# Gate and up projections: weight loads that read every second word in half of the contraction groups

## The chip, the cores and the metric

The kernel runs on one core of a Trainium2 chip. The metric is the device time of one execution, in microseconds (us). The kernel before takes 2003.84 us, the median of 2 runs (2003.69 and 2003.99). The engines are named as in the profile: PE is the matrix engine TensorE, PEld its weight loads, DVE the VectorE, ACT the ScalarE, POOL the GpSimd, SP the SyncE, which here only issues transfers.

## The reference

One layer of a decoder trunk with 512 tokens and 2048 features, all in float32: a norm, an input projection, two groups of attention heads side by side, an output projection, a residual sum, and then the part that this case is about, a gated feed-forward block with 5632 inner features.

```python
def _swiglu(h, w_gate, w_up, w_down):
    return (jax.nn.silu(h @ w_gate) * (h @ w_up)) @ w_down

def reference(x, ...):
    for l in range(DEPTH):
        h = _rms_norm(x, attn_norm[l])
        x = x + _hybrid_mixer(h, ...)
        h = _rms_norm(x, ffn_norm[l])
        x = x + _swiglu(h, w_gate[l], w_up[l], w_down[l])
    return x
```

Here `w_gate` and `w_up` are 2048 x 5632 and `w_down` is 5632 x 2048.

## The kernel before

**Products.** Each float32 operand is cut into a high and a low part by ScalarE (a copy that rounds) and VectorE (the difference), and a product of two operands is taken as three products on TensorE: high by high, high by low, low by high. Gate, up and down also use a scheme with seven products of sums of blocks in place of eight products of blocks (a Strassen-like scheme), so the operands are "forms", seven sums of blocks each.

**Gate and up.** The output features of each of the two matrices are cut into 22 pairs of blocks of 128 (`NJ`, index `j`), and the 2048 features that are summed over into 4 contraction groups (`NG`, index `g`). For each `j`, first gate and then up (`which`) runs over its four groups. Step `i` stands for one group, so there are 22 x 2 x 4 = 176 steps. The weights of a step come from HBM in one transfer of 512 KB into a tile `r`, as four blocks of 256 words on each of 128 partitions: two halves (`kk`) of 128 words each, one behind the other. VectorE adds the blocks to the forms (`sums`), and ScalarE and VectorE write the high and low parts of all seven forms into the tile `bigm` (`part_steps`), at one of two places in turn. The activations' forms lie ready for the whole stage: the program names them forma for group 0, formx for group 1, formy for group 2, and for group 3 they lie in bigm as well.

A step then makes 42 matmuls: for the high part of the weights 2 halves x 7 forms x 2 (the activations' high and low part), and for the low part 2 halves x 7 forms. Each has 256 tokens as its columns, and each is preceded by a weight load of its own, 128 x 128, even where two matmuls in a row use the same weights. In the profile a matmul is PE, its load PEld. The weights are the stationary operand:

```python
cs = slice(kk * P, (kk + 1) * P)
...
mm(o, w[wp][:, fb, cs], a[:, xp, fa], ...
```

The helper `mm` (line 412) reads the moving operand not one column after the other, but in turn from the two halves of the block: column 0, column 128, column 1, column 129 and so on. Attention's products (`mm3`) call the engine directly and read their columns one after another. No stationary operand is read in any other way than word after word.

The results gather in four PSUM tiles `q`. After four steps they are put together by VectorE and ScalarE (`evict`, `gate_out`, `up_out`) while the next matrix is running, and the finished blocks go to HBM for the last stage.

**Down** follows as the last stage, with 512 columns in each matmul (tiles `pd`).

**Order of the work.** Up to the start of the second pair of gate the order on each engine is written out in a table (`ORDERS`); behind it the program's own order holds. TensorE runs the steps one after the other; the sums and the parts of a step are made one and two steps ahead, and the transfers are issued three to four steps ahead on SP.

**The functions and their use.** `_blocks` lays out the two matrices on the host, `kernel` calls it, and `hybrid_layer` holds the loop.

Of the kernel before, what the change touches and what calls it, by code (L numbers as in the profile page):

```python
# [18 lines left out]
P = 128  # L19
# [9 lines left out]
NG = 4  # L29
# [204 lines left out]
def hybrid_layer(ctx: ExitStack, tc: tile.TileContext, xT, vec, ffb, wfg, wfirst, win, cmpw, wout, wos, wgu, wdn, out):  # L234
# [109 lines left out]
    def split(dst, src, scale=None, neg=None):  # L344

        if scale is None:
            h = act(dst[:, 0], src, AF.Copy)
            tt(dst[:, 1], src, dst[:, 0].bitcast(F32), op=OP.subtract)
            return h
        else:  # L350
            sca.activation(dst[:, 0], src, AF.Copy, scale=scale)
            dve.scalar_tensor_tensor(dst[:, 1], src, scale, dst[:, 0].bitcast(F32),
                                           op0=OP.mult, op1=OP.subtract)
# [14 lines left out]
    def high_tile(name):  # L368
        return wpl.tile([P, HALF * P], FR, tag="wh", name=name, bufs=2)
# [42 lines left out]
    def mm(o, w, x, j=1, **kw):  # L412
        pe.matmul(_like(o, j), w, _in_turn(x, j), **kw)
# [17 lines left out]
    def stagger(*gens, lag=LAG):  # L431

        for g in gens:
            for i, mark in enumerate(g):
                if mark is POST:
                    run(late[0])
                    late[0] = g
                    break
                if i >= lag and i % 2 == 0:
                    next(late[0], None)  # L440
                yield

    def run(steps):
        for _ in steps:
            pass
# [603 lines left out]
    def chain(*gens):  # L1049
        for g in gens:  # L1050
            yield from g
# [12 lines left out]
    for k in range(NK):  # L1064
# [5 lines left out]
        wp = high_tile(f"w0p_{k}")[:, :2 * T].rearrange("p (s c) -> p s c", s=2)  # L1070
# [134 lines left out]
    def fetch(at):  # L1205
        key = next(wanted, None)
        if key is None:
            if at < 3:
                ws_turn.append(at)
            return  # L1210
        n, f = key
        while emitted[0] < GROUP * (n // 2 + 1):
            sum_weights(highs[-1], osums)
            emitted[0] += 1
        i = FIRST7 + 2 * n
        src = {0: win[i, 0], 1: win[i, 1], 6: win[i + 1, 1]}.get(f)
        if src is None:
            src = fsum[PAIRS[n]][{4: 0, 3: 1, 5: 2, 2: 3}[f]].rearrange("p i c -> p (i c)")
        fetched[key] = ws_tile(f"pair{n}_{f}", at), at
        load(fetched[key][0], src)  # L1220
# [156 lines left out]
    for n, p in enumerate(PAIRS[:-1]):  # L1377
        g = stagger((pair if p[0] == "p" else vpair)(p[1]), lag=LAG7)
# [67 lines left out]
    def x1_steps(n, z, place=None, formed=False):  # L1446

        xr = ftile(f"xr{n}") if place is None else oxp.tile([P, T], F32, tag="ox", name=f"xr{n}", bufs=OXB)
        load(xr, xT[n])
        t, sq = (ftile(f"x1_{n}"), xr) if place is None else (xr, place)  # L1450
        yield
        tt(_apart(t, 2), _mixed(z[0], 2), _apart(xr, 2), op=OP.add)
        pin(sca.dma_start(x1d[n], t)) if n == NK - 1 else pool.dma_start(x1d[n], t)
        yield
        if formed:
            raw_forms(n, t)
        add_squares()
        act(sq, t, AF.Square)
        squared.append((n, sq))
        if formed:  # L1460
            yield
            add_squares()
        yield
# [112 lines left out]
    for i, n in enumerate((0, HALF)):  # L1576
        g = x1_steps(n, both_z[i:])
# [3 lines left out]
    for n, tag, at in ((5, "g", 4),):  # L1581
        z = [None, tag]
        pieces += [one_tile(n, z, j) for j in range(2)]
        g = x1_steps(n, z)
# [15 lines left out]
    def seven_out(p):  # L1600

        n = SEVEN[p]
        c = [oxp.tile([P, T], F32, tag="ox", name=f"c7_{n}{i}", bufs=OXB) for i in range(2)]
        xs = [x1_steps(n + HALF * i, c[i:], c[i]) for i in range(2)]
        for x in xs:
            next(x)
        yield
        steps = put_together(qs[p], c, ftile(f"e7_{n}"))
        next(steps)
        yield  # L1610
        next(steps)
        yield
        run(steps)
        next(xs[0])
        yield
        next(xs[1])
        yield
        next(xs[0])
        yield
        next(xs[1])  # L1620
        yield

    for g in order7:
        at = len(pieces)
        pieces += g
        if g in others:
            p = others.index(g)
            o = seven_out(p)
# [7 lines left out]
    for i, n in enumerate((5 + HALF, 6, 6 + HALF, 7, 7 + HALF)):  # L1636
# [3 lines left out]
        def tail(n=n, z=z):  # L1640
            x = x1_steps(n, z, formed=(n % HALF == 7))
            if n == 7 + HALF:
                live["x1s"] = x
            next(x)
            yield
            next(x)
            yield
            if n == 7:
                next(x)
                live["raw7"] = live["raw"]  # L1650
            next(x)
            yield

        g = tail()
# [139 lines left out]
    ORDER = list(range(2 * NJ * NG))  # L1794
# [14 lines left out]
    def sums(i):  # L1809
        r = raws[i]  # L1810
        tt(r[:, 4:6], r[:, 1:3], r[:, 0:1].to_broadcast([P, 2, 256]), op=OP.add)
        tt(r[:, 6], r[:, 4], r[:, 2], op=OP.add)
        tt(r[:, 7], r[:, 6], r[:, 3], op=OP.add)
# [14 lines left out]
    def parts(i):  # L1828
        run(part_steps(i))
# [79 lines left out]
    def load_a(i):  # L1909
        second, j = pass_of(i)[1:]  # L1910
        at = (8 + 2 * (turn[1] % 3)) * T
        turn[1] += 1
        rawa[i] = cut(live["fa"], at, (3 if second else 4) * 256)
        d = fetch2(rawa[i], ad[j][:, 4:7] if second else ad[j][:, 0:4])
        if i == 2:
            tc.add_manual_dep(d.ins, live["w0"].ins.name, PACE)
# [53 lines left out]
    for j in range(NJ):  # L1970
        for which in range(2):
            q = [ps.tile([P, T], F32, tag=tag, name=f"q{which}{j}_{i}", bufs=BUFS[tag])
                 for i, tag in enumerate(SETS[which])]
            for g in range(NG):
                i = (2 * j + which) * NG + g

                if 3 <= i < LAST - 1:
                    sums(i + 2)
                if 3 <= i < LAST:
                    parts(i + 1)  # L1980
                    fetch(i + 4)
                if i == 4:
                    split(fr2, acc)
                if i == LAST - 2:
                    live["fa"] = ffp.tile([P, 2 * FORM + OFF_FORM], F32, tag="fa", name="rawm", bufs=1)
                    for n in range(2):
                        load_a(n)
                        run(load_w(n))
                w = split_w.pop(i)
                if j == 1 and which == 0 and g == 0:  # L1990
                    close_order(tc, engines)

                for wp in range(2):
                    for kk in range(2):
                        k = 2 * (ORDER[i] % NG) + kk
                        a = forms[k]
                        cs = slice(kk * P, (kk + 1) * P)
                        for fa, fb, b, h in PROD:
                            o = q[b][:, h * 256:(h + 1) * 256]
                            for xp in range(2 - wp):  # L2000
                                mm(o, w[wp][:, fb, cs], a[:, xp, fa],
                                   start=(k == 0 and h == 0 and wp == 0 and xp == 0),
                                   stop=(g == NG - 1 and kk == 1 and wp == 1), skip_group_check=True)
                if i == 0:
                    sums(2)
                    form_sums(live["raw"])
                    parts(2)
                    sums(3)
                    form_parts(HALF - 1, live["raw"])
                elif i == 1:  # L2010
                    sums(4)
                    parts(3)
                    run(x1s)
                    fetch(5)
                elif i == 2:
                    fetch(6)
                if j == 0 and which == 1 and g == 1:
                    row_rstd2([sets[0][3][:, 256:512], q[3][:, 256:512]])
                next(pending, None)
                if g == 1 and j > 0:  # L2020
                    next(turning, None)
                if i >= LAST - 1:
                    ahead[i - LAST + 1] = splits(i - LAST + 1)
            sets = [q]
            pending = chain(pending, (up_out if which else gate_out)(j, q))
# [94 lines left out]
    for ps_ in range(4):  # L2120
        p, second = ps_ // 2, ps_ % 2
# [71 lines left out]
        pending = chain(*ends)  # L2193


def _in_turn(x, j=1):

    return x.rearrange("p (j b a) -> p j a b", j=j, b=2)


def _like(x, j=1):

    return x.rearrange("p (j a b) -> p j a b", j=j, b=2)
# [24 lines left out]
def _blocks(w, np):  # L2228

    w = w.reshape(2, NG, 2, P, -1, 2, P)  # L2230
    w = np.stack([w[0, ..., 1, :], w[0, ..., 0, :], w[1, ..., 1, :], w[1, ..., 0, :]])
    return np.ascontiguousarray(w.transpose(4, 1, 3, 0, 2, 5)).reshape(-1, NG, P, 4 * 2 * P)
# [75 lines left out]
```

## Time and profile before

| | |
|---|---|
| median of the timed runs | 2003.84 us |
| the profiled execution | 2001.04 us, of which its span is 1999.3 us |
| granted TensorE clock | 1.0 |
| PE busy | 1989.7 us (100% of the span), 14413 matmuls |
| PEld busy | 1883.6 us (94%), 14413 loads |
| DVE busy | 1783.7 us (89%) |
| ACT busy | 1098.6 us (55%) |
| POOL busy | 332.8 us (17%) |
| matmuls into q | 4 x 1848, 275 ns each |
| weight loads for q | 4 x 1848, 192 ns each |
| matmuls into q, first and last start | 768.6 and 1596.3 us of the span |

How to read it: the rows name the tile written and, behind the arrow, the tiles read. All operations have line 195, that of a helper which records them, so groups are told apart by tiles. A matmul's duration is modelled and neighbouring matmuls overlap, and so do loads; the pace of TensorE is therefore read from the starts of the instructions, not from their durations. The rows give the shape of a load, but not the step at which it reads.

### The profile page before, as it was taken

The page shows a single profiled execution, that of the slowest core. Times are in us where ns is not written, and L with a number is a line of the kernel's source. Part 1 is how long each engine was busy: PE and PEld are TensorE (multiplying, and loading weights), DVE is VectorE, ACT ScalarE, POOL GpSimd, SP SyncE. Part 2 cuts the span into 40 slices and gives each one's busy share as a digit, 9 for nine tenths or more (in the row PEclk, how much of TensorE's full clock was granted, in tenths as well). Part 3 has the DMA queues.
Part 4 walks back from the last instruction along what each step waited for, and adds up shares of the span by engine and source line. Part 5 has one row for each costly group of instructions (what it writes and reads, how often), then busy time and mean ns, then how long its engine had stood idle before and what let it go on. Part 6 is the DMA issues. An engine that isn't in the chain of part 4 may idle for free.

```text
span 1999.3 us, 36667 instructions
## 1 busy us (share of the span) xinstructions
PE 1989.7 (100%) x14413; PEld 1883.6 (94%) x14413; DVE 1783.7 (89%) x2733; ACT 1098.6 (55%) x1466; POOL 332.8 (17%) x497
## 2 busy tenths in 40 slices
PE   9999999999999999999999999999999999999999
PEld 8988989899999999999999999999999988888888
DVE  7778779888889779999999999999999997888897
ACT  6656656668797465444444443443444455566574
POOL 1032343433230010111111111111111000001000
PEclk9999999999999999999999999999999999999999
DMA  6686787978884783677777867777767698579974
GB/s 215 225 194 161 191 188 187 233 207 240 259 259 160 249 265 129 192 209 222 210 209 223 215 200 217 209 213 216 207 195 213 207 354 284 157 237 322 354 199 142
DMA packets 156287, 438.18 MB, mean 219 GB/s; under 512 B 19081, under 2 KB 27273, under 8 KB 156114
## 3 DMA queue, kind: packets, MB, share of 16 engines
q1 hardware_dynamic: 102608, 299.17, 45.1%
q0 software_dynamic: 46352, 110.39, 25.5%
q10 hardware_dynamic: 7154, 26.27, 3.5%
q8 instruction: 113, 1.85, 0.4%
q14 instruction: 60, 0.49, 0.1%
HBM read 399.30 MB, written 132.93 MB: 266 GB/s over the span
## 4 chain that ended last, share of the span: by engine, by line
PE 95%; DVE 3%; ACT 1%; DMA 0%; issue 0%; SPq 0%; ACTq 0%; DVEq 0%
PE q L195 40%; PE pd L195 20%; PE po L195 7%; PE ps_kf L195 6%; PE ps_qn L195 4%; PE ps_vf L195 4%; PE ps_vs L195 2%; PE ps_first L195 2%; PE on L195 2%; PE ps_kw L195 1%; PE ps_qf L195 1%; PE s_s L195 1%; PE ps_ks L195 1%; PE s_w L195 1%; PE s_f L195 1%; PE of L195 1%
## 5 line engine op out<-in xcount | busy, mean ns | idle before, releaser
L195 ACT ACTIVATE bigm<-r 128x1792 fp32r<-128x1792 f32 x174 | 299.6, 1722 | 392.6 <-PE q L195 195.8
L195 DVE TENSOR_TENSOR bigm<-r,bigm 128x1792 fp32r<-128x1792 f32 x174 | 351.1, 2018 | 0.1
L195 DVE TENSOR_TENSOR r<-r 128x512 f32<-128x512 f32 x522 | 265.8, 510 | 22.8 <-DMA r<-wgu 11.3
L195 POOL DMA_DIRECT2D wsum<-wdn x176 | 120.3, 695 | 669.4 <-ACT bigm L195 588.6
L195 PE MATMUL q<-formx,bigm 128*128 128x256 f32 x1848 | 213.6, 275 | 1.1 <-ACT bigm L195 1.1
L195 PE MATMUL q<-forma,bigm 128*128 128x256 f32 x1848 | 213.6, 275 | 0.3 <-ACT bigm L195 0.3
L195 PE MATMUL q<-formy,bigm 128*128 128x256 f32 x1848 | 213.5, 275 | 0.0
L195 PE MATMUL q<-bigm 128*128 128x256 f32 x1848 | 213.5, 275 | 0.0
L195 PEld LDWEIGHTS q<-formx,bigm 128*128 128x128 f32 x1848 | 209.9, 192 | 1.3 <-ACT bigm L195 1.3
L195 PEld LDWEIGHTS q<-forma,bigm 128*128 128x128 f32 x1848 | 210.0, 192 | 0.5 <-ACT bigm L195 0.5
L195 PEld LDWEIGHTS q<-formy,bigm 128*128 128x128 f32 x1848 | 209.9, 192 | 0.0
L195 PEld LDWEIGHTS q<-bigm 128*128 128x128 f32 x1848 | 209.9, 192 | 0.0
L195 PE MATMUL pd<-bigm 128*128 128x512 f32 x900 | 202.4, 379 | 0.0
L195 PEld LDWEIGHTS pd<-bigm 128*128 128x128 f32 x900 | 170.1, 189 | 24.1
L195 DVE TENSOR_TENSOR bigm<-wd,bigm 128x1024 fp32r<-128x1024 f32 (+1 forms) x62 | 107.6, 1736 | 20.8 <-ACT bigm L195 20.7
L195 ACT ACTIVATE bigm<-wd 128x1024 fp32r<-128x1024 f32 (+1 forms) x62 | 90.8, 1465 | 31.7 <-DMA wd<-wsum 26.5
L195 ACT ACTIVATE bigm<-rawm 128x768 fp32r<-128x768 f32 (+2 forms) x72 | 65.7, 922 | 63.7 <-PE pd L195 37.9
L195 PE MATMUL pd<-bigm,formx 128*128 128x512 f32 x444 | 99.3, 379 | 0.0
L195 PEld LDWEIGHTS pd<-bigm,formx 128*128 128x128 f32 x444 | 83.9, 189 | 11.9
L195 DVE TENSOR_TENSOR bigm<-rawm,bigm 128x768 fp32r<-128x768 f32 (+2 forms) x72 | 75.5, 1057 | 16.7 <-ACT bigm L195 16.2
L195 PE MATMUL po<-bigm,wp_o 128*128 128x512 f32 (+1 forms) x448 | 83.2, 336 | 0.0
L195 POOL DMA_DIRECT2D fsump<-win x72 | 48.7, 746 | 176.9 <-ACT wp_ks L195 45.8
(499 smaller groups left out, 3810.8 us busy)
## 6 DMA issues: line engine op xcount, KB each, us to landing
r<-wgu SPq DMA_DIRECT2D x174, 512.0 KB, 3.7
wsum<-wdn POOLq DMA_DIRECT2D x176, 256.0 KB, 5.1
rawm<-ad SPq DMA_DIRECT2D x44, 512.0 KB, 7.8
wd<-wdn SPq DMA_DIRECT2D x40, 512.0 KB, 6.4
wd<-wsum SPq DMA_DIRECT2D x40, 512.0 KB, 7.2
ad<-cb ACTq DMA_DIRECT2D x22, 896.0 KB, 5.8
fsump<-win POOLq DMA_DIRECT2D x72, 256.0 KB, 4.8
rawm<-ad SPq DMA_DIRECT2D x44, 384.0 KB, 3.5
```

The costliest lines, as they stand in the source:

```text
L195: r = f(*args, **kw)
```

## The change

In the odd contraction groups (1 and 3) of gate and up, the host lays the two halves of each block of 256 words in turn: word 0 of the first half, word 0 of the second, word 1 of the first, and so on. Where the weights are read as the stationary operand, the groups with odd numbers take every second word (a step of two words, eight bytes) from an even or an odd start; the groups with even numbers read 128 neighbouring words as before. What lies in TensorE after the load is the same, and so are the results. Sums and parts are made element by element and don't know of the order. The number, order, shape and size of all instructions and transfers stay as they are.

```diff
                             for xp in range(2 - wp):
-                                mm(o, w[wp][:, fb, cs], a[:, xp, fa],
+                                mm(o, _stationary(w[wp][:, fb], ORDER[i] % NG, kk), a[:, xp, fa],
                                    start=(k == 0 and h == 0 and wp == 0 and xp == 0),
...
+def _stationary(x, g, kk):
+
+    return x.rearrange("p (a k) -> p k a", k=2)[:, kk] if g % 2 else x[:, kk * P:(kk + 1) * P]
+
+
+def _laid(w, np):
+
+    v = w.reshape(*w.shape[:-1], 4, 2, P)
+    o = v.copy()
+    for g in (1, 3):
+        o[:, g] = v[:, g].swapaxes(-1, -2).reshape(o[:, g].shape)
+    return o.reshape(w.shape)
...
-        "wgu": np.stack([_blocks(f(w_gate), np), _blocks(f(w_up), np)]),
+        "wgu": np.stack([_laid(_blocks(f(w_gate), np), np), _laid(_blocks(f(w_up), np), np)]),
```

`ORDER[i] % NG` is the number of the contraction group of step `i` (the last two steps of the stage are exchanged).

## The prediction

> **What bounds the kernel now.** I read the page first, for its busy times and its chain.
>
> ```profile
> span 1999.3 us, 36667 instructions
> ...
> PE 1989.7 (100%) x14413; PEld 1883.6 (94%) x14413; DVE 1783.7 (89%) x2733; ACT 1098.6 (55%) x1466; POOL 332.8 (17%) x497
> ...
> PE 95%; DVE 3%; ACT 1%; DMA 0%; issue 0%; SPq 0%; ACTq 0%; DVEq 0%
> ...
> L195 PE MATMUL q<-formx,bigm 128*128 128x256 f32 x1848 | 213.6, 275 | 1.1 <-ACT bigm L195 1.1
> L195 PE MATMUL q<-bigm 128*128 128x256 f32 x1848 | 213.5, 275 | 0.0
> ...
> r<-wgu SPq DMA_DIRECT2D x174, 512.0 KB, 3.7
> ```
>
> TensorE is the chain for 95% of the span. The products that the change touches write the tiles q. There are 4 x 1848 = 7392 of them, each with a weight load of its own, and the name behind the arrow tells the contraction group: forma is group 0, formx 1, formy 2, bigm alone 3. The second answer is the table of busy times for the stage of gate and up and a full stretch inside it.
>
> ```profile
> core 0: us, PE busy (x) PEld busy (x) DVE busy (x) ACT busy (x) POOL busy (x), PEclk, DMA share, GB/s
> 768.40:1601.90 833.50, 832.13 (x7424) 831.05 (x7423) 803.39 (x1084) 353.87 (x258) 120.33 (x176) 1.00 0.72 207
> 1000.00:1200.00 200.00, 200.00 (x1794) 200.00 (x1793) 190.68 (x259) 81.98 (x58) 31.47 (x47) 1.00 0.74 211
> ```
>
> The stage is 833.5 us long, at a granted clock of 1.00, and TensorE has no idle time in it beyond 1.4 us. VectorE is busy 803.4 us, so it has 30 us to spare; the others have far more. Busy time doesn't say what sets TensorE's own pace, since pipelined instructions overlap. The order of time in the middle of the stage does (start, length from the first start to the last end, engine, count).
>
> ```profile
> 1000.75 4.85 PE L195 MATMUL q<-formx,bigm 128*128 128x256 f32 x42
> 1005.44 4.85 PE L195 MATMUL q<-formy,bigm 128*128 128x256 f32 x42
> 1010.13 4.85 PE L195 MATMUL q<-bigm 128*128 128x256 f32 x42
> 1000.64 4.77 PEld L195 LDWEIGHTS q<-formx,bigm 128*128 128x128 f32 x42
> 1005.33 4.77 PEld L195 LDWEIGHTS q<-formy,bigm 128*128 128x128 f32 x42
> ```
>
> Matmul groups start 4.69 us apart, and so do the loads: 4.69 / 42 = 111.7 ns for a load and its matmul, in odd and even groups alike. 7392 x 111.7 ns = 825.7 us of the 833.5.
>
> Which of the two sets the 111.7 ns? A matmul alone: in the last stage 512 columns are taken at a time.
>
> ```profile
> 1800.99 5.34 PE L195 MATMUL pd<-bigm,formx 128*128 128x512 f32 x24
> 1806.17 4.05 PE L195 MATMUL pd<-bigm 128*128 128x512 f32 x18
> L195 PEld LDWEIGHTS pd<-bigm 128*128 128x128 f32 x900 | 170.1, 189 | 24.1
> L195 PEld LDWEIGHTS q<-bigm 128*128 128x128 f32 x1848 | 209.9, 192 | 0.0
> ```
>
> 5.18 / 24 = 215.8 ns for 512 columns, 0.4215 ns a column; 256 columns would need 107.9 ns. A load alone comes from loads of other widths (partitions x columns, mean ns behind the busy time):
>
> ```profile
> L195 PEld LDWEIGHTS ps_cum<-tri,lfr 128*8 128x8 f32 x8 | 0.6, 88 | 0.5
> L195 PEld LDWEIGHTS zr_kc<-zs_kc,rows 128*64 128x64 f32 x2 | 0.3, 134 | 0.1
> L195 PEld LDWEIGHTS pcT<-ident,pc 128*96 128x96 f32 x32 | 3.7, 126 | 0.7
> L195 PEld LDWEIGHTS pT_s<-ident,p_s 128*128 128x128 f32 x80 | 9.9, 141 | 1.7
> ```
>
> From 8 to 128 columns a load grows from 88 to 189 ns: 101 / 120 = 0.84 ns a column, and some 81 ns that don't depend on the width. Of a load of 192 ns in q, 111 ns are thus its columns, which is the pace of 111.7 ns. So in q the loads set the pace, and the matmuls, with a floor of 107.9, follow closely. What a load gains or loses in q reaches the end of the span, up to 3.8 ns of gain and without limit in loss.
>
> **The change, part by part.** The instruction lists of the five engines are row for row the same before and after; no DMA, wait or buffer moves.
>
> *On the host* the words of the blocks of 256 are put in another order. That costs the device nothing: `r<-wgu` still moves 512 KB a time in whole rows. VectorE's sums and the copies to high and low parts work element by element on whole blocks, in the shapes they had: 0.
>
> *The weight loads* of groups 1 and 3 read 128 words at a step of two words instead of one. These are 22 column pairs x 2 matrices x 2 groups x 42 = 3696 loads, and all are on the path. The trace has no stationary operand read at a step, so the price is bounded from both sides.
>
> Below nothing: the shortest load in this tile took 186 ns against 192, and a load that is shorter by 6 ns leaves the matmul's 107.9 ns as the pace: -3.8 ns x 3696 = -14 us. The row is the tile's own:
>
> ```profile
> L195 PEld LDWEIGHTS q<-formx,bigm x1848: 186/192/192, 774.5 to 1586.8; 128*128 128x128 f32 x185
> ```
>
> (minimum, median and maximum stand behind the count.) Above: the load slows to half its rate, because it has twice the memory to cross: 0.84 ns more a column, 107.5 ns a load x 3696 = +397 us.
>
> What speaks for a value near 0 is that this read path is not at its limit. The loads for transposes (pT, pcT) also take words of four bytes, and grow by 141 - 126 = 15 ns for 32 columns: 0.47 ns a column, or (141 - 81) / 128 = 0.47. The path can therefore deliver a word in 0.47 ns where a load of q asks for one in 0.84, so a step costs nothing as long as the price goes by words. If memory is fetched in pieces of k neighbouring words, a step of two doubles the pieces per word: one in k/2 x 0.84 = 0.42k ns, where the transposes' loads get one in 0.47k. That is 12% more than they show, but they may not have asked for more. I take 0, by the words.
>
> So it is less clear whether reading at that rate of pieces is free of small stalls. The moving operand shows some. In most products its columns are read in turn from the two halves of a block, word by word; in attention they are read one after another. The rows of the two kinds, of attention (on) and of the value projection (wl), whose next rows start at 156.02 and 75.92:
>
> ```profile
> 155.33 0.85 PE L195 MATMUL on<-pt_w,vs 128*128 128x512 f32 x3
> 156.02 0.81 PE L195 MATMUL ps_qn<-bigm,wp_qn 128*128 128x512 f32 x3
> 74.97 1.12 PE L195 MATMUL ps_vs<-wl_vs,bigm 128*128 128x256 f32 x8
> 75.92 0.27 PE L195 MATMUL z_kc<-wp_kc,qq 128*128 128x256 f32 x1
> ```
>
> 0.69 / 3 = 230 ns for 512 columns read one after another, against 215.8 in turn: 6.6% more. 0.95 / 8 = 118.8 ns for 256, against 107.9: 10% more. The transposes' loads, at 0.47 ns against 0.4215, are 11.5% above the best pace of a word too. So in this trace a plain sequence at 0.42 ns a word is the slower pattern, and a load of q at a step of two passes through memory as fast as such a sequence does. A stall of 6.6 to 11.5% of 107.5 ns is 7 to 12 ns a load, 26 to 46 us in all; I keep that as a rival.
>
> The Trainium skill, "SBUF — State Buffer", section "Door 1: The DMA port swizzle", says that memory has lines of 16 bytes and that at least two consecutive hits on a line give full bandwidth, while each access to a new line costs something. By its first half a step of two words of four bytes, with two hits a line, is free, and the sum would be 0. The trace doesn't bear out the second half for the moving operand: in turn, where every word lies on another line than the word before it, is the faster pattern (215.8 against 230 ns), which the rule tells the other way round.
>
> *What would be late next.* If the loads of odd groups were slower, VectorE, the input transfers and ScalarE get more time per group and nothing of theirs grows. If they were faster, a pair of groups falls from 2 x 4.69 to 4.69 + 4.53 us (42 x 107.9), 4.61 on average; VectorE needs 190.68 / 200 of 4.69 = 4.47, so it would not take over.
>
> The sum against the profiled execution, 2001.04 us (1999.3 of span and 1.7 around it): 0 + 0 + 0 = 2001. The two timed runs have a median of 2003.84, which is 2.8 above it; the change keeps that distance, and the forecast in their terms is 2003.8.
>
> **The rivals.**
>
> *The load's rate falls with the step* (slower). Mechanism: the load path fetches a fixed piece of neighbouring words for each step, and uses half of what it fetches, or has a quick form for a step of one only. Place: the 3696 loads of formx and bigm groups. Price at half the rate: pace 111.7 + 107.5 = 219.2 ns, +397 us, 2401 us. It decides, that is passes 2% (40.1 us), from 40.1 / 3696 = 10.8 ns a load. For it: loads in q are bound by reading, with nothing to hide a longer one, and no load at a step is in the trace, so it can't be excluded. Against it: the 0.47 ns a word of the transposes' loads, and a moving operand that jumps with every word at full pace. The Trainium skill, "TensorE: Matmul & The Clock Gate", section "Weight-path perf modes", has a fast weight load that isn't used for 32-bit weights, so by that page there is no quick form to lose; no run here shows it. Chance 0.16.
>
> *Small stalls of a sequence at the pace of pieces* (a little slower): 26 to 46 us, at 9% of 107.5 ns or 9.7 ns some 36 us: 2040. For it: three rows with 6.6, 10 and 11.5%. Against it: those words are asked for one in every 0.42 ns, and the load asks for half as many; in turn, with as many words, shows no stall. The penalty for each access to a new line that the Trainium skill has ("SBUF — State Buffer", the section above) would act like this, since a load then changes lines twice as often. Chance 0.22, and in one such case of three more than 2%.
>
> *The step spares the load something* (a little faster): 3 to 6 ns a load as in pd (189) or the shortest of q (186), up to -14 us: 1990 to 1993. For it: in turn is the quicker pattern for the moving operand. Against it: 192 in nearly every load of q, whichever buffer the operands lie in, looks like a fixed pace of issue. Chance 0.07.
>
> *The change doesn't do what it says*, because the loads are made with a step of one over words that were laid out anew on the device: no row speaks for it, and the access is in the code (0.01); the time would be 2004.
>
> **How the numbers follow.** Forecast, no change, 0.54: 2003.8, with 3 us on either side. Rate falls 0.16, stalls 0.22, gain 0.07, the rest 0.01. Forecast, stalls and gain hold 0.83, so the range reaches from the full gain, 2003.8 - 14 = 1990, to the dearest stall, 2003.8 + 46 = 2050, and leaves the halved rate out. 2%, about what a measurement of this kernel can tell from no change, is 40 us. Slower by over 2%: 0.16 + 0.22 / 3 = 0.23. Faster by over 2%: the matmul's floor caps the gain at 0.7%, so 0.01 for what I haven't seen. Within 2%: 0.76.
>
> **What would show it.** The even groups are a control inside the same run. Right: the groups formx and bigm still start 4.69 us apart, with loads of 192 ns, and q's stage lasts 833 us. Stalls: the groups of formx and bigm take 5.0 to 5.2 us and those of forma and formy 4.69, with loads that vary by some ns. Halved rate: 9.2 us for an odd group, loads near 300 ns, VectorE's share of the stage down to two thirds. Gain: 4.53 us for an odd group and loads of 186 to 189 ns. Wrong altogether would be a change in the groups of forma and formy, or outside q's stage, since nothing there is touched.

## The result, and the profile after

The changed kernel takes 2026.52 us (median of 2 runs, 2026.08 and 2026.96) against 2003.84, which is 22.7 us or 1.13% more. The ratio on record is 1.0124, with a 95% interval of 1.0108 to 1.014, that is 21.6 to 28.1 us: a change that stands clear of its interval though it stays within 2%. The forecast was 2003.8; the time is inside the stated range of 1990 to 2050, some 3 us below the place of the second rival (2030 to 2050).

The order of time in the middle of the stage, now (start, length, engine, tiles, count):

```profile
1002.39 4.85 PE L195 MATMUL q<-forma,bigm 128*128 128x256 f32 x42
1007.08 5.13 PE L195 MATMUL q<-formx,bigm 128*128 128x256 f32 x42
1012.05 4.85 PE L195 MATMUL q<-formy,bigm 128*128 128x256 f32 x42
1016.74 5.13 PE L195 MATMUL q<-bigm 128*128 128x256 f32 x42
1021.71 4.85 PE L195 MATMUL q<-forma,bigm 128*128 128x256 f32 x42
```

The groups that weren't touched still last 4.69 us (1002.39 to 1007.08, 1012.05 to 1016.74). The two with a step last 4.97 us: 118.3 ns for a load and its matmul in place of 111.7. 3696 x 6.65 ns = 24.6 us. The whole span grew by 2025.3 - 1999.3 = 26.0 us, so 1.4 us are left over for the rest of the program, which is no more than the runs of one kernel differ by (2000.57 to 2002.65 for seven runs of the kernel before, beside the first experiments).

From the page and the list of the tile's instructions (minimum, median, maximum of a duration behind the count):

```profile
span 2025.3 us, 36667 instructions
...
PE 2013.6 (99%) x14413; PEld 1908.1 (94%) x14413; DVE 1788.1 (88%) x2733; ACT 1093.3 (54%) x1466; POOL 331.8 (16%) x497
...
L195 PEld LDWEIGHTS q<-forma,bigm x1848: 189/192/192, 768.6 to 1605.8; 128*128 128x128 f32 x185
L195 PEld LDWEIGHTS q<-formx,bigm x1848: 194/197/201, 774.7 to 1610.7; 128*128 128x128 f32 x185
L195 PEld LDWEIGHTS q<-bigm x1848: 196/196/201, 784.3 to 1615.7; 128*128 128x128 f32 x185
```

The loads with a step record 196 to 197 ns instead of 192. That is less than the 6.65 ns by which the pace grew: a load's recorded duration doesn't show its whole price, and the starts do. VectorE is busy 1788.1 us against 1783.7, hardly more, so the loss wasn't handed on to it.

### The profile page after: what moved, and what is told of

The parts are those of the page before. It is cut to its first block, busy times and chain, and to the rows that moved or that the text cites. A ratio compares the mean times of both kernels' runs of the same rounds, so it can differ in the third digit from the quotient of the medians.

```text
span 2025.3 us, 36667 instructions
## 1 busy us (share of the span) xinstructions
PE 2013.6 (99%) x14413; PEld 1908.1 (94%) x14413; DVE 1788.1 (88%) x2733; ACT 1093.3 (54%) x1466; POOL 331.8 (16%) x497
## 4 chain that ended last, share of the span: by engine, by line
PE 93%; DVE 3%; DMA 1%; issue 1%; ACT 1%; SPq 0%; ACTq 0%; DVEq 0%
PE q L195 42%; PE pd L195 16%; PE po L195 7%; PE ps_kf L195 6%; PE ps_qn L195 4%; PE ps_vf L195 4%; PE ps_first L195 2%; PE ps_vs L195 2%; PE on L195 2%; DMA wd<-wsum 1%; PE ps_kw L195 1%; PE ps_qf L195 1%; PE ps_ks L195 1%; PE s_s L195 1%; PE s_w L195 1%
## 5 line engine op out<-in xcount | busy, mean ns | idle before, releaser
L195 POOL DMA_DIRECT2D wsum<-wdn x176 | 120.4, 696 | 691.7 <-ACT bigm L195 579.1
L195 PE MATMUL q<-formx,bigm 128*128 128x256 f32 x1848 | 225.9, 282 | 1.1 <-ACT bigm L195 1.1
L195 PE MATMUL q<-bigm 128*128 128x256 f32 x1848 | 225.9, 282 | 0.0
L195 PEld LDWEIGHTS q<-formx,bigm 128*128 128x128 f32 x1848 | 222.1, 197 | 1.2 <-ACT bigm L195 1.2
L195 PEld LDWEIGHTS q<-bigm 128*128 128x128 f32 x1848 | 222.3, 197 | 0.0
```

The costliest lines, as they stand in the source:

```text
L195: r = f(*args, **kw)
```

## The experiments

Two theories lead. A, lines: an operand of TensorE is fetched from memory in lines of 4 words (16 bytes), and a stream of words that needs one line after another gets a new line every 1.78 ns at best, whatever it uses of it. B: the reads of the two operands meet now and then, and the step only changes where. C, that distance itself costs, was kept beside them. The 1.78 ns is worked out from the result itself: 111.7 ns less 107.5 for the columns leaves 4.2 ns that don't go by columns, and (118.3 - 4.2) / 64 lines = 1.78. So a step of two words is no test of A; other steps are. Where no ratio is given, a time below is that of one run, and the readings rest on the paces inside it, in most of these runs beside an unchanged group 0. The kernel before ran beside each set, with medians of 2001.1 to 2001.6 us in these sets.

**Steps 1 to 4.** Each group has a step of its own:

```diff
+STEPS = (1, 2, 3, 4)
...
-    return x.rearrange("p (a k) -> p k a", k=2)[:, kk] if g % 2 else x[:, kk * P:(kk + 1) * P]
+    s = STEPS[g]
+    x = x.rearrange("p f c -> p (f c)")
+    at = min(fb * 256 + kk * P, 7 * 256 - P * s)
+    return x[:, at:at + P * s].rearrange("p (a k) -> p k a", k=s)[:, 0] if s > 1 else x[:, at:at + P]
```

> The loads of groups 0, 1, 2 and 3 read at a step of 1, 2, 3 and 4 words (where the block of 256 words is too short for that, they go on into the next blocks, so the products of groups 1 to 3 are of other weights than the layer's: only the times mean something). Theory A, lines: a load takes its words from lines of 4 words (16 bytes), one line after another, and each new line takes at least 1.78 ns (114.1 ns for the 64 lines of a load at step 2, that is the pace of 118.3 ns less 4.2 ns that don't depend on the columns). Then step 3 touches 96 lines and has a pace of 96 x 1.78 + 4.2 = 175 ns, step 4 touches 128 lines and has 232 ns: groups of 42 last 4.69, 4.97, 7.35 and 9.74 us, the whole kernel some 2355 us. Theory B, the two reads meet: a load at a step collides now and then with the moving operand's reads, a matter of a few ns; steps 3 and 4 stay between 112 and 125 ns, the kernel under 2060 us. Theory C, distance: each word of step adds 6.6 ns: 111.7, 118.3, 125 and 131.5 ns, 2080 us.

Measured: 2355.14 us, against 2355 by theory A, 2060 at most by B and 2080 by C. The order of time, groups 1, 2, 3 and then 0:

```profile
1016.44 5.13 PE L195 MATMUL q<-formx,bigm 128*128 128x256 f32 x42
1021.41 7.46 PE L195 MATMUL q<-formy,bigm 128*128 128x256 f32 x42
1028.71 10.03 PE L195 MATMUL q<-bigm 128*128 128x256 f32 x42
1038.57 4.85 PE L195 MATMUL q<-forma,bigm 128*128 128x256 f32 x42
```

From start to start 4.97, 7.30 and 9.86 us, or 118.3, 173.8 and 234.8 ns a load; expected by lines were 118.3, 175 and 232. Less the 4.2 ns (an estimate), a line costs 114.1 / 64 = 1.78, 169.6 / 96 = 1.77 and 230.6 / 128 = 1.80 ns. That the total agrees to the microsecond is in part luck, since step 3 is 1.2 ns a load quicker and step 4 2.8 ns slower than A has it. B and C fall.

**Steps 6, 8 and 12.** The same with `STEPS = (1, 6, 8, 12)`.

> The same with steps of 1, 6, 8 and 12 words in groups 0 to 3 (other weights than the layer's in groups 1 to 3). Theory A, lines: from step 4 on each word lies on a line of its own, so all three cost the same, 128 lines, 232 ns, groups of 9.74 us; the kernel some 2004 + 3 x 44 x 5.05 = 2670 us. Theory B: under 125 ns everywhere. Theory C, distance: 145, 158 and 184 ns, growing with the step.

2736.63 us, against some 2670 by theory A; group 3 (step 12), then 0, 1 and 2:

```profile
1007.54 11.37 PE L195 MATMUL q<-bigm 128*128 128x256 f32 x42
1018.75 4.85 PE L195 MATMUL q<-forma,bigm 128*128 128x256 f32 x42
1023.44 9.68 PE L195 MATMUL q<-formx,bigm 128*128 128x256 f32 x42
1032.95 10.24 PE L195 MATMUL q<-formy,bigm 128*128 128x256 f32 x42
1043.04 2.30 PE L195 MATMUL q<-bigm 128*128 128x256 f32 x8
```

9.51 us, 226.4 ns, for step 6; 10.09 us, 240.2 ns, for step 8; 11.21 us, 266.9 ns, for step 12. The steep climb from 2 to 4 words has ended, as 4 words to a line demand: three times the distance, from step 4 to step 12, costs 32 ns, where from step 2 to 4 alone it was 116.5. But one pace for all, as A had it, is not what was measured: step 6 comes to (226.4 - 4.2) / 128 = 1.74 ns a line, a little under the 1.78 that A calls the best, and 8 and 12 are dearer than a line each explains.

**Both reads changed.** In the changed kernel, groups 2 and 3 read the moving operand one column after another:

```diff
-                                mm(o, _stationary(w[wp][:, fb], ORDER[i] % NG, kk), a[:, xp, fa],
+                                (mm if ORDER[i] % NG < 2 else pe.matmul)(o, _stationary(w[wp][:, fb], ORDER[i] % NG, kk), a[:, xp, fa],
```

> The changed kernel, but in groups 2 and 3 the moving operand's 256 columns are read one after another in place of in turn (so the tokens come out in another order there, and the sums in q are no longer the layer's). Group 0: step 1 and in turn; 1: step 2 and in turn; 2: step 1 and one after another; 3: step 2 and one after another. Theory A, lines, each read with a stream of its own: 111.7; 118.3; 64 lines of the moving operand, 118 ns; and both at once no more than the slower of the two, 118 to 119 ns, as they run side by side. Theory B, the two reads meet: a collision needs both, so group 3 is unlike the other three, either the sum of both losses (125 ns or more) or none (112 ns).

2031.06 us. Groups 1, 2, 3, 0:

```profile
1007.75 5.13 PE L195 MATMUL q<-formx,bigm 128*128 128x256 f32 x42
1012.72 4.94 PE L195 MATMUL q<-formy,bigm 128*128 128x256 f32 x42
1017.50 5.21 PE L195 MATMUL q<-bigm 128*128 128x256 f32 x42
1022.55 4.85 PE L195 MATMUL q<-forma,bigm 128*128 128x256 f32 x42
```

118.3 ns with the load at a step alone; 4.78 us or 113.8 ns with the moving operand one after another alone, which is 64 lines at 1.778 ns with nothing added; 5.05 us or 120.2 ns with both. Each read has a cost of its own: the step costs a load 6.6 ns beside the one way of reading the moving operand (118.3 - 111.7) and 6.4 beside the other (120.2 - 113.8). In the main the two reads overlap, but A allowed no more than the slower of them, 118.3, and that is 1.9 ns too little: what the two lose above 111.7 adds up, 6.6 + 2.1 = 8.7 ns against 8.5 measured. B's sum of both losses was put at 125 with 118 for the moving operand alone, which was too dear; with the 113.8 measured it is 120.4. So this run doesn't speak against B. What does are steps 3 and 4, which cost far more than collisions of a few ns, and the last stage below, where a load at a step of two costs the matmul beside it nothing. Why the two losses add up stays open.

**All four groups.** `_stationary` and `_laid` take every group in place of the odd ones.

> The change in all four groups, so twice the loads at a step of two (7392), with the layer's own result. If the loss goes by loads, whatever their group and place, it doubles: 2 x 22.7 = 45 us, 2049 us, all groups 4.97 us long. If it came from the odd groups' place (their weights always lie in the second of two places, which is what theory B could turn on), groups 0 and 2 stay at 4.69 us and the time at 2027 us.

2049.38 us, ratio 1.0239 (1.0222 to 1.0256) to a median of 2001.62 in the same set: 47.8 us for 7392 loads, or 6.5 ns a load. All groups last 4.97 us; groups 0, 1 and 2:

```profile
1010.16 5.13 PE L195 MATMUL q<-forma,bigm 128*128 128x256 f32 x42
1015.13 5.13 PE L195 MATMUL q<-formx,bigm 128*128 128x256 f32 x42
1020.10 5.13 PE L195 MATMUL q<-formy,bigm 128*128 128x256 f32 x42
```

So the loss goes by loads, and the odd groups' place plays no part.

**Patterns of the moving operand, one stream.** Loads as before, and in groups 1 to 3:

```diff
+    elif g == 1:
+        pe.matmul(o, w, two.rearrange("p (a k) -> p k a", k=2)[:, 0], **kw)
+    elif g == 2:
+        pe.matmul(o.rearrange("p (a b) -> p a b", b=2), w, two.rearrange("p (a k b) -> p k a b", k=2, b=2)[:, 0], **kw)
+    else:
+        pe.matmul(o.rearrange("p (a b) -> p a b", b=4), w, two.rearrange("p (a k b) -> p k a b", k=2, b=4)[:, 0], **kw)
```

(`two` are 512 neighbouring words.)

> The kernel before with its plain loads; only the moving operand's 256 columns are read in other patterns (of other words than the layer's in groups 1 to 3, so the sums aren't the layer's). Group 0: in turn from two halves as before. Group 1: one stream at a step of two words, 128 lines. Group 2: two words, then two left out, 128 lines. Group 3: four words, then four left out, 64 lines. If the cost of a stream goes by its lines, at 1.777 ns each (64 lines took 113.7 ns for columns read one after another in the run with both reads changed), the paces are 111.7 (the loads'), 227.5, 227.5 and 113.7 ns, and groups of 42 last 4.69, 9.55, 9.55 and 4.78 us. If it goes by the step between words, group 2 is quicker than group 1, and group 3 slower than columns one after another.

2444.09 us. Groups 1, 2, 3, 0:

```profile
1004.94 9.80 PE L195 MATMUL q<-formx,bigm 128*128 128x256 f32 x42
1014.57 9.81 PE L195 MATMUL q<-formy,bigm 128*128 128x256 f32 x42
1024.20 5.09 PE L195 MATMUL q<-bigm 128*128 128x256 f32 x42
1029.12 4.85 PE L195 MATMUL q<-forma,bigm 128*128 128x256 f32 x42
```

A step of two words and two words of every four cost the same 9.63 us, 229.3 ns or 1.79 ns for each of 128 lines. Four words of every eight cost 4.92 us, 117.1 ns, for 64 lines. So it isn't the step between words that is paid for but, in the main, the number of lines. 117.1 is 3.3 ns above the 113.8 of 64 neighbouring lines, which stays unexplained.

**Patterns of the moving operand, two streams.** In turn from two halves at a step of two words (group 1), in turn from two neighbouring lines (group 2), one after another (group 3):

```diff
+    elif g == 1:
+        pe.matmul(_like(o), w, two.rearrange("p (b a k) -> p k a b", k=2, b=2)[:, 0], **kw)
+    elif g == 2:
+        pe.matmul(o.rearrange("p (a c b) -> p a c b", c=4, b=2), w, one.rearrange("p (a b c) -> p a c b", c=4, b=2), **kw)
+    else:
+        pe.matmul(o, w, one, **kw)
```

> The kernel before with its plain loads; the moving operand's columns again in other patterns (tokens in another order or other words in groups 1 to 3, so the sums aren't the layer's). Group 0: in turn from two halves as before, 64 lines. Group 1: in turn from two halves, at a step of two words in each, 128 lines. Group 2: in turn from two neighbouring lines (word 0, 4, 1, 5, ...), 64 lines. Group 3: one after another, 64 lines. If two lines are fetched side by side when the words come from two of them in turn, group 1 is well below 227.5 ns (113.7 if the fetches overlap wholly, so that the pace is 114 to 120), and group 2 has the loads' 111.7. If each line costs its 1.777 ns whatever the order, group 1 has 227.5 and group 2 113.7 like group 3, and group 0's 111.7 stays unexplained.

2016.82 us. Groups 1, 2, 3, 0:

```profile
1004.87 5.12 PE L195 MATMUL q<-formx,bigm 128*128 128x256 f32 x42
1009.83 4.85 PE L195 MATMUL q<-formy,bigm 128*128 128x256 f32 x42
1014.51 4.95 PE L195 MATMUL q<-bigm 128*128 128x256 f32 x42
1019.30 4.85 PE L195 MATMUL q<-forma,bigm 128*128 128x256 f32 x42
```

In turn from two places, 128 lines take 4.96 us, 118.1 ns, where one stream took 229.3 for as many. From two neighbouring lines in turn the pace is the loads' (4.68 us). One after another it is 4.79 us, 114.0 ns. That is what two lines fetched side by side would give when the words are asked for in turn; the overlap is inferred from the pace. It would be why this kernel's products, read so, don't show the price of lines that attention's show.

**A load at a step beside 512 columns.** In the last stage, all 1848 loads at a step of two:

```diff
-mm(b[t][2 * k + h], a[xp][:, fa, t * P:(t + 1) * P], w[0][:, fb],
+mm(b[t][2 * k + h], _every(a[xp], fa, t), w[0][:, fb],
```

> The kernel before, with gate and up untouched; all 1848 loads of the last stage (down, 512 columns a matmul, pace 215.8 ns) read at a step of two words. Tokens come out in another order there, so the output isn't the layer's. Line theory: such a load needs 118 ns, and the matmul beside it 215.8, so nothing is lost: the pace stays at 215.8 ns and the time within 3 us of before. If a load at a step slows the matmul it runs beside, as well, the loss of 6.6 ns a load shows here too: 12 us.

2001.09 us, ratio 1.0003 (0.9993 to 1.0013): nothing. From the order of time and from the groups by shape (mean ns of one load behind the busy time):

```profile
1800.21 5.34 PE L195 MATMUL pd<-bigm,formx 128*128 128x512 f32 x24
1805.39 6.85 PE L195 MATMUL pd<-bigm 128*128 128x512 f32 x31
L195 PEld LDWEIGHTS pd<-bigm 128*128 128x128 f32 x900 | 177.1, 197 | 17.4 <-ACT bigm L195 0.3
```

5.18 / 24 = 215.8 ns as before, with loads of 197 instead of 189 ns. The load is slower here too, and hidden.

**The same with a step of four.**

> The same with a step of four words in all loads of the last stage (other words than the layer's activations there). Line theory: the load's 235 ns, measured in gate and up, pass the matmul's 215.8 by 19.2 ns, x 1848 = 35 us: the pace is 235 ns and the kernel takes some 2037 us. If a load at a step only delays what it runs beside, by a few ns, it stays under 2015 us.

2042.93 us, 41.6 more than the 2001.36 beside it. Order of time and loads:

```profile
1799.75 4.45 PE L195 MATMUL pd<-formx,bigm 128*128 128x512 f32 x18
1804.04 4.45 PE L195 MATMUL pd<-bigm 128*128 128x512 f32 x18
L195 PEld LDWEIGHTS pd<-bigm 128*128 128x128 f32 x900 | 219.3, 336 | 0.0
```

4.29 / 18 = 238.3 ns; (238.3 - 215.8) x 1848 = 41.6 us. Where the load outlasts the matmul, what it has too much is paid in full. 238.3 is 3.5 ns above the 234.8 of gate and up, so 35 us was too small; why is open.

**Steps 5, 7, 10 and 13**, to see what makes 8 and 12 dear.

> Loads at steps of 5, 7, 10 and 13 words in groups 0 to 3 (other weights than the layer's). Each word lies on a line of its own, so by lines alone all have one pace; steps 4, 6, 8 and 12 gave 235, 227, 240 and 267 ns, which lines alone don't explain. Theory D, parts of the memory that are taken in turn: steps that aren't multiples of 4 words spread over more parts, so 5, 7, 10 and 13 stay at 226 to 235 ns. Theory E, distance: the pace grows with the step on top of the lines, so 13 words have 267 ns or more and 10 words some 250.

2921.38 us. Groups 0 to 3 and the next 0:

```profile
1006.21 9.68 PE L195 MATMUL q<-forma,bigm 128*128 128x256 f32 x42
1015.73 10.09 PE L195 MATMUL q<-formx,bigm 128*128 128x256 f32 x42
1025.65 9.69 PE L195 MATMUL q<-formy,bigm 128*128 128x256 f32 x42
1035.18 10.94 PE L195 MATMUL q<-bigm 128*128 128x256 f32 x42
1045.96 9.67 PE L195 MATMUL q<-forma,bigm 128*128 128x256 f32 x42
```

Step 5: 226.7 ns, step 7: 236.2, step 10: 226.9, step 13: 256.7. Neither expectation holds: 13 isn't a multiple of 4 and is dear, and 10 is further than 7 and 8 and is cheap.

**The steps in other groups**: 12, 8, 6 and 4 words in groups 0 to 3.

> Loads at steps of 12, 8, 6 and 4 words in groups 0 to 3, the earlier steps in other groups and against other tiles of activations (other weights than the layer's). If the pace belongs to the step, it is 267, 240, 227 and 235 ns again, and groups of 42 last 11.2, 10.1, 9.5 and 9.9 us. If it came from the group's place in memory or from the moving operand beside it, the numbers stay with the groups instead.

2960.07 us. Groups 3 (step 4), 0 (12), 1 (8), 2 (6) and 3 again:

```profile
1001.48 10.05 PE L195 MATMUL q<-bigm 128*128 128x256 f32 x42
1011.37 11.37 PE L195 MATMUL q<-forma,bigm 128*128 128x256 f32 x42
1022.57 10.24 PE L195 MATMUL q<-formx,bigm 128*128 128x256 f32 x42
1032.65 9.63 PE L195 MATMUL q<-formy,bigm 128*128 128x256 f32 x42
1042.12 10.05 PE L195 MATMUL q<-bigm 128*128 128x256 f32 x42
```

235.5, 266.7, 240.0 and 225.5 ns: each pace belongs to its step, within 1 ns. What singles out 7, 8, 12 and 13 words stays open.

## Why the prediction was wrong, point by point

**What bounds the stage** was right. The loads set the pace, at 111.7 ns, and what a load lost reached the end: 24.6 us in the groups that were changed, all of it in the span, and nothing in the groups beside them. The last stage shows the same from the other side, with nothing lost as long as the matmul's 215.8 ns outlast the load.

**The step that failed** is the price of the weight loads, "I take 0, by the words". The transposes' loads were read as proof that the path gives a word every 0.47 ns and so has room to spare at 0.84. What the runs show in its place is a price by lines: one line of four words every 1.78 ns, so that a step of two needs 64 lines or 114 ns where the load's columns took 107.5, and 6.65 ns x 3696 = 24.6 us were lost in place of 0. By lines, 0.47 ns a word is 4 x 0.47 = 1.88 ns a line, close to that limit and no spare capacity. (That the transposes' loads are themselves held by it wasn't tested; their 0.47 comes from recorded durations.) The prediction had worked out that a step of two asks for a piece in 0.42k ns where the transposes get one in 0.47k, and passed over it with "they may not have asked for more". The row of attention it quoted gives the measured pace nearly as it stands: 230 / 128 = 1.80 ns a line, x 64 lines, + 4.2 = 119 ns, or 7.5 ns x 3696 = 28 us. With the 1.778 ns that 64 lines of the moving operand gave, measured apart from the load's 118.3, it is 118.0.

**The second rival** (stalls of a sequence, 0.22) was the case, with its reason: a load at a step of two passes through memory as fast as columns that are read one after another. Its price of 26 to 46 us was a little high. The low end, from attention's 6.6%, is 7.1 ns a load and comes near the 6.65 measured. The upper end came from the 11.5% of the transposes' loads, and the 10% between them from 118.8 ns for 256 columns in a short run of eight, which take 113.8 in a long run. It is also no stall but a steady rate, and so its "loads that vary by some ns" was only half seen: from 194 to 201 ns, nearly all 196 to 198, in a pattern that repeats with every group. The forecast itself missed; the range held the time because it was drawn to take in this rival.

**The first rival** (the rate falls with the step) named a right mechanism, "fetches a fixed piece of neighbouring words for each step, and uses half of what it fetches", with a wrong price. A load at a step of one uses so little of the path (by the 1.78 ns an estimated 32 x 1.78 = 57 ns of 107.5) that doubling its lines costs 6.65 ns and not 107.5. Its other mechanism, a quick form for a step of one only, would be paid once; it doesn't explain the climb from step 2 to 4 (118.3, 173.8 and 234.8 ns).

**The gain** and the change that does nothing were excluded by the even groups as a control: 4.69 us against 4.97 in one and the same run.

**The Trainium skill's rule**, "SBUF — State Buffer", section "Door 1: The DMA port swizzle", was read in the prediction as saying that two hits on a line of 16 bytes are enough. The size of the line is borne out: the steep climb of the price ends at a step of four words. Two hits are not enough: by 1.78 ns a line, two words at the load's 0.84 ns cover 1.68, and the 0.1 ns that is missing, times 64 lines, is the 6.6 ns lost. For the moving operand even four hits are too few (4 x 0.4215 = 1.69 ns). And a new line with each access shows no price when the moving operand is read in turn from two lines: the pace stays the loads' (111.7 ns).

## What to carry to other kernels

Count the 16-byte lines that each operand of a matmul touches, at 1.78 ns a line for one stream (for a moving operand read in turn from two places it was about half, 118.1 / 128 = 0.92), and compare it with what the other operand needs. The longer of the two sets the pace, though not to the nanosecond: where both were near the limit, 1.9 and 3.5 ns came on top, and with each word on a line of its own the loads' pace was 225 to 267 ns by the step. A stationary operand at a step of two words is free beside 512 moving columns and costs 6.6 ns a load beside 256; at a step of four words it costs 123 ns beside 256 and 22 beside 512. When a page's row shows a path at a rate, ask in which unit the rate is limited before calling the distance to it spare.

## What the runs showed that was not expected

- A moving operand that asks for words in turn from two places gets its lines twice as fast, as if two were fetched side by side, even where each word's neighbour is left out: 128 lines in 118.1 ns against 229.3 in one stream.
- What a load at a step and a moving operand read one column after another lose adds up (6.6 + 2.1 ns against 8.5), though the two reads overlap in the main. The cause is open.
- With each word on a line of its own, a load's pace still depends on the step: 225 to 227 ns at 5, 6 and 10 words, 235 at 4, 236 at 7, 240 at 8, 257 at 13, 267 at 12. The cause is open.
- The pace of the slowed loads repeats from group to group, 4.97 us each time in the rows above and in nearly all other odd groups of the stage, with ScalarE, VectorE and the transfers working beside it. Nothing here points to contention with them.
